# A two-layer diffusion backbone on one core: one adaLN sum a round in the first stage, attention biases asked for six units ahead, probabilities scaled on ScalarE, row norms with one PSUM bank per quarter and six chunks apart

## The chip, the cores and the metric

The kernel runs on one core of one Trainium2 chip. The metric is device time in microseconds (us). A core has five engines that run beside each other, each in its own order: TensorE (PE, with PEld for its weight loads), VectorE (DVE), ScalarE (ACT), GpSimd (POOL) and SyncE (SP). SP here does nothing but issue DMAs. An engine's queue is strictly in order, so an instruction that waits holds everything behind it. PSUM has eight banks of 512 fp32 numbers per partition.

## The reference

Two layers over 256 latent tokens of width 2048, with 256 context tokens. All is fp32.

- For each layer, six vectors come from `silu(cond) @ ada_w + ada_b` (adaLN): shift, scale and gate for the mixer, and the same for the FFN. Layer 0 needs shift and scale for latent tokens and for context tokens.
- Layer 0: `hx = rmsnorm(x) * g * (1 + scale) + shift`, the same for the context; Q, K, V and three convolution inputs from one projection; eight heads of neighbourhood attention. A query's scores are `q k / sqrt(128)` plus a relative position bias within its window, and plain scores for the 256 context keys; softmax over both; times V. Beside it a gated width-3 convolution. Both go through `w_out`, times the gate, onto x. Then a SwiGLU FFN (hidden width 5632) with its own norm and modulation.
- Layer 1: the same with a spatial-gating MLP in the place of attention. At the end an rmsnorm.

## The kernel before

**Products.** Every fp32 product is made of three fp32r products: each operand is split into a high part (`hi`, a copy by ScalarE that rounds) and a low part (`lo`, VectorE subtracts `hi`), and `mm3` (L172 to L175) issues hi by hi, hi by lo, lo by hi. Weights arrive as 512 KB chunks `raw` (four buffers), SP issues them, ScalarE makes `hl0`, VectorE makes `hl1` (six buffers each).

**First stage, 16 rounds** (the loop `for g in range(17)`, from L1092). A round loads four adaLN weight tiles `adaw` of 512 KB (`ada_tile`), a K chunk (512 KB) and a half V chunk (256 KB). TensorE multiplies the tiles by the two conditioning vectors (`row_part`, L336, into `aps`); VectorE copies the sums out (`asb`, L349); TensorE turns them into columns (`to_cols`, L362, `cps`). Rounds 0 to 7 make the scales and scale the inputs (`scale_step`); rounds 8 to 15, called shift rounds here, make the shifts and add them (`shift_step`, L415: a chain POOL, VectorE, ScalarE, VectorE for each of four pieces). In between TensorE multiplies the chunk of the round before, in four parts (`kv_part`). The 17th pass has only parts. The x and context columns are loaded by `load_x` at the rounds in `X_AT`; `row_sums` and `row_norms` make the row norms in round 6.

**The other adaLN sums.** The remaining ten sections are not products on TensorE: VectorE multiplies a 512 KB tile by silu(c) and sums it (`ada_compute`, L222). 320 such tiles are spread over the kernel by a running account (`ada["due"]`): `RATE_SH` tiles a shift round, `RATE_V1`, `RATE_EARLY` and `RATE_LATE` afterwards. They share a pool of three buffers (`adap`) with the first two of a round's four tiles.

**After that, units.** A unit is one weight chunk times one half of the tokens (t = 0 or 1): six matmuls. Chunks follow each other, t = 0 then t = 1. Around each of the three boundaries at which a row norm stands (before FFN 0, before the gMLP, before FFN 1) the last `LAG` chunks run for t = 0 and then for t = 1, and the first `LAG` of the next block likewise, so that a norm of one half has `LAG` units of the other half to hide in. Splits are emitted some 8 units ahead of their use, loads 13.

**Helpers that advance by units.** Attention, norms and evacuations are generators: each `yield` is one unit. `norm_T` takes one half's rows times their norm (`n`), turns each of four 512-wide quarters on TensorE (`flip`, T) and, in `fill` (E), applies scale and shift out of PSUM, 128 columns at a time: two by ScalarE (L791), two by VectorE (L793), into `hs`, and splits that into `tf`. `NORM_SEQ` lists which T and E stand in which step. `attention(h, t)` asks at t = 0 for the head's bias tile (`bias_tile`, two DMAs by SP with rows of 64 numbers, and a mask added by POOL, L688), waits three units, and then makes scores (`s`), adds the bias on VectorE (L701), takes the maximum, exponentials, reciprocals of the sums, and scales the probabilities on VectorE (L712); three units later TensorE transposes them (`pt`, L515). `ATT_AT` gives the units at which the 16 half heads start.

Of the kernel before, what the change touches and what calls it, by code (L numbers as in the profile page):

```python
# [32 lines left out]

LAG = 5
TW, TWA = 4, 3
HI_LEAD, DMA_LEAD, LEAD_IN = 8, 13, 14
RATE_SH, RATE_V1, RATE_EARLY, RATE_LATE = 1.5, 1.25, 0.88, 0.6
HOMES = {0: (1, 2, 1, 2), 1: (0, 0, 0, 1), 2: (0, 0, 1, 2)}  # L40
LEAD_AT = range(-14, -8), range(-8, -3), range(-3, 0)
X_AT = {0: (0,), 1: (1, 2), 2: (3, 4), 3: (5, 6), 4: (7,)}
FIRST_WAIT, KV_WAIT, X1_WAIT, ROW_WAIT = 2, 3, 4, 6
QUIET, LN_QUIET = (10, 5), (32, 39)
N_SPARE, SPARE_LEAD = 2, 12
# [3 lines left out]
def seq(text):  # L49
    return [[(a[0], int(a[1])) for a in step.split()] for step in text.split(",")]  # L50


NORM_SEQ = seq("T0 T1, E0 E1, T2 T3, E2 E3"), seq("T0, E0 T1, E1 T2, E2 T3, E3")
ACT_N = 1,
ATT_AT = (20, 6), (83, 5)
B_RAW, B_HL, B_ADA, B_STG = 4, 6, 3, 7


# [1 line left out]
def tile_backbone(  # L60
# [53 lines left out]
    def tp_tile(name):  # L114
        return tpp.tile([P, 512], F32, tag="tp", name=name)
# [572 lines left out]
        nc.gpsimd.tensor_tensor(out=ball, in0=ball, in1=mask.unsqueeze(1).to_broadcast([P, 6, GRID]), op=ALU.add)  # L688

    def attention(h, t):  # L690
        if t == 0:
            bias_tile(h)
            for _ in range(3):
                yield
        bias = BIAS[h][:, 2 - 2 * t:6 - 2 * t]
        sp = tp_tile("s")
        nc.tensor.matmul(sp, QT[h // 4, t][:, 128 * (h % 4):128 * (h % 4) + 128], kT(h), start=True, stop=True)
        yield
        s = stage("s")
        nc.scalar.copy(s[:, 256:512], sp[:, 256:512])  # L700
        nc.vector.tensor_tensor(out=s[:, 0:256], in0=sp[:, 0:256], in1=bias.rearrange("p r c -> p (r c)"),  # L701
                                op=ALU.add)
        yield
        mx = tiny.tile([P, 1], F32, tag="mx", name="mx")
        nc.vector.tensor_reduce(out=mx, in_=s, axis=AX.X, op=ALU.max, negate=True)
        yield
        sm = tiny.tile([P, 1], F32, tag="sm", name="sm")
        nc.scalar.activation(s, s, AF.Exp, bias=mx, accum_out=sm)
        yield
        rs = tiny.tile([P, 1], F32, tag="rs", name="rs")  # L710
        nc.vector.reciprocal(rs, sm)
        nc.vector.tensor_scalar(s, s, rs, None, op0=ALU.mult)  # L712
        yield from wait(TWA)
        tp = transpose4(s, "pt")
        yield
        pt = stage("pts")
        copy(h, pt, tp)
        yield from wait(TWA)
        av = tp_tile("av")
        for i in range(4):  # L720
            nc.tensor.matmul(av[:, 0:128], vv(h, i), pt[:, 128 * i:128 * i + 128],
                             start=(i == 0), stop=(i == 3))
        yield
        dh, dl = (MIX[0][:, k, h, 128 * t:128 * t + 128].rearrange("p (r c) -> p r c", c=GRID) for k in range(2))
        hi_part(dh, rev(av[:, 0:128], 2))
        yield
        lo_part(dl, rev(av[:, 0:128], 2), dh)
# [35 lines left out]
    def norm_T(key, t, l, part, T):  # L763
        assert ada["done"] >= 32 * (1 + max(ada_plan.index((l, sec)) for sec in ((0, 1), (3, 4))[part == "ffn"]))
        r = rms(key, t)
        ns = [stage("n") for _ in range(4)]
        for q in range(4):
            xq = X1[0][:, t, 512 * q:512 * q + 512]
            if q in ACT_N:
                nc.scalar.activation(ns[q], xq, AF.Copy, scale=r)  # L770
            else:
                nc.vector.tensor_scalar(ns[q], xq, r, None, op0=ALU.mult)
        for _ in range(NORM_WAIT):
            yield
        tps = {}

        def flip(q):
            tps[q] = [tp_tile("ntp")[:, 0:256] for _ in range(2)]
            for j in range(4):
                nc.tensor.transpose(tps[q][j // 2][:, 128 * (j % 2):128 * (j % 2) + 128],  # L780
                                    ns[q][:, 128 * j:128 * j + 128], ident)

        def fill(q):
            h, lw = quad(T, 4 * q, t)
            hs = stage("hs").rearrange("p (i k t) -> p i k t", i=2, k=2)
            for j in (0, 2, 1, 3):
                kt = 4 * q + j
                a, b = A[l, part][:, kt:kt + 1], SH[l, part][:, kt:kt + 1]
                src = tps[q][j // 2][:, 128 * (j % 2):128 * (j % 2) + 128]
                if j < 2:  # L790
                    nc.scalar.activation(hs[:, 0, j], src, AF.Identity, bias=b, scale=a)  # L791
                else:
                    nc.vector.tensor_scalar(hs[:, 1, j - 2], src, a, b, op0=ALU.mult, op1=ALU.add)  # L793
            for k in range(2):
                ks = slice(2 * k, 2 * k + 2)
                hi_part(h[:, ks], hs[:, k])
                lo_part(lw[:, ks], hs[:, k], h[:, ks])

        for step in NORM_SEQ[t]:
            for what, q in step:  # L800
                (flip if what == "T" else fill)(q)
            yield
# [71 lines left out]
    T1 = []  # L874
# [192 lines left out]
            if next(g, gens) is gens:  # L1067
                gens.remove(g)

    att_at = {}  # L1070
    for half, (u, step) in enumerate(ATT_AT):
        for k in range(8):
            att_at[4 * N_V1 + u + step * k] = (4 * half + k // 2, k % 2)

    quiet = [(b - QUIET[0], b + QUIET[1]) for b in bounds[:-1]]
    quiet.append((bounds[1] + LN_QUIET[0], bounds[1] + LN_QUIET[1]))
# [22 lines left out]
    for g in range(17):  # L1099
# [9 lines left out]
        if blk:  # L1109
# [1 line left out]
            for q in range(4):  # L1111
                row_part(aps, tiles[q], 4 * q)
            asb = row_done(aps, 256)
        if g >= 8:
            while ada["loaded"] < min(ada["done"] + 1, 14):
                ada_load()
        if g == 4:
            nc.gpsimd.dma_start(s_b, c_row.partition_broadcast(P))
        if g > 0:
# [1 line left out]
        if g == 16:  # L1121
            for u in LEAD_AT[1]:
                leads(u)
        if blk:
            cps = to_cols(asb, 2)
            if g == 0:
                pair = [split_tiles(r) for r in raw]
                held[0] = [[w.rearrange("p (j n) -> p j n", j=2) for w in p] for p in pair]
                scale_step(g, cps, [lambda j=j: [split_half(r, p, j) for r, p in zip(raw, pair)] for j in range(2)])
            elif g < 8:  # L1130
                scale_step(g, cps)
            else:
                shift_step(g - 8, cps, rb)
            if g > 0:
                held[g] = [split(r) for r in raw]
        if g > 1:
            kv_part(4 * g - 3)
        if g == 6:
            diag = row_sums()
        if g > 1:  # L1140
            kv_part(4 * g - 2)
        if g > 0:
            kv_part(4 * g - 1)
        if g == 6:
            rb = row_norms(diag)
        for s in X_AT.get(g, ()):
            squares(s)
# [2 lines left out]
        if 8 <= g < 16:  # L1150
            ada_ticks(RATE_SH)
        if g == 15:
            for u in LEAD_AT[0]:
                leads(u)
    KV[1] = big_f32("kv1")
# [1 line left out]
    kv_done(*acc_ps[1], ks1, 256)  # L1157
    for u in LEAD_AT[2]:
        leads(u)
    nc.vector.tensor_copy(cpad[:, :, 0:2], Sm)  # L1160

    for u in range(len(units)):
        leads(u)
# [4 lines left out]
        go(run(ci, t, hi, lo))  # L1168
        if i + 1 in starts:
            go(starts[i + 1](t))  # L1170
        if u in att_at:
            go(attention(*att_at[u]))
        if not any(a <= i < b for a, b in quiet):
# [76 lines left out]
```

## Time and profile before

| | |
|---|---|
| three runs | 2372.53 us median, 2369.86 to 2373.77 |
| the profiled execution | 2374.91 us, of which the trace's span is 2373.1 us |
| PE busy | 2311.2 us, 97% of the span |
| VectorE, ScalarE, GpSimd busy | 1611.7, 1009.6, 85.1 us |
| moved by DMA | 623.45 MB, 263 GB/s on average |
| granted TensorE clock, mean | 0.992 of full speed |

The profile is read from TensorE outwards: a busy PE at a full granted clock can't be helped by this change, so what counts is where PE is idle, where its clock is below 1.00, and which wait ends last there. Start times are in us from the start of the span. "A <- B" is an operation that writes A and reads B.

### The profile page before, as it was taken

The page shows a single profiled execution, that of the slowest core. Times are in us where ns is not written, and L with a number is a line of the kernel's source. Part 1 is how long each engine was busy: PE and PEld are TensorE (multiplying, and loading weights), DVE is VectorE, ACT ScalarE, POOL GpSimd, SP SyncE. Part 2 cuts the span into 40 slices and gives each one's busy share as a digit, 9 for nine tenths or more (in the row PEclk, how much of TensorE's full clock was granted, in tenths as well). Part 3 has the DMA queues.
Part 4 walks back from the last instruction along what each step waited for, and adds up shares of the span by engine and source line. Part 5 has one row for each costly group of instructions (what it writes and reads, how often), then busy time and mean ns, then how long its engine had stood idle before and what let it go on. Part 6 is the DMA issues. An engine that isn't in the chain of part 4 may idle for free.

```text
span 2373.1 us, 29680 instructions
## 1 busy us (share of the span) xinstructions
PE 2311.2 (97%) x11022; PEld 1883.9 (79%) x11022; DVE 1611.7 (68%) x2171; ACT 1009.6 (43%) x1268; POOL 85.1 (4%) x109
## 2 busy tenths in 40 slices
PE   8988999999999999999999999999999999999998
PEld 5766777778788888888888788887888888888886
DVE  4554579889776777777777778777774554455445
ACT  4322245444544434443444545446444344444443
POOL 3121000000000000000000000000000000000001
PEclk9998999999999999999999999999999999999999
DMA  9666888889688888878877688885876665655563
GB/s 353 239 248 244 295 278 281 279 307 362 222 292 313 307 297 323 310 287 305 325 289 286 209 300 321 281 299 183 317 272 216 204 192 182 194 195 190 183 195 133
DMA packets 184113, 623.45 MB, mean 263 GB/s; under 512 B 25952, under 2 KB 32288, under 8 KB 183584
## 3 DMA queue, kind: packets, MB, share of 16 engines
q1 hardware_dynamic: 181840, 614.71, 73.7%
q0 software_dynamic: 1840, 6.33, 0.8%
q8 instruction: 86, 1.41, 0.2%
q10 hardware_dynamic: 288, 0.52, 0.1%
q14 instruction: 59, 0.48, 0.1%
HBM read 619.35 MB, written 2.13 MB: 262 GB/s over the span
## 4 chain that ended last, share of the span: by engine, by line
PE 87%; DVE 5%; DMA 4%; issue 2%; ACT 1%; POOL 1%; SPq 0%; POOLq 0%; ACTq 0%; DVEq 0%
PE mm L173 25%; PE mm L175 25%; PE mm L174 25%; DMA bias<-in_rpb_dram 3%; DVE hl L522 1%; PE k L173 1%; PE k L174 1%; PE k L175 1%; PE aps L336 1%; DMA adaw<-in_ada_sh_dram 1%; DVE adaw L222 1%; PE htp L515 1%; PE v L173 1%; PE v L174 1%; PE v L175 1%
## 5 line engine op out<-in xcount | busy, mean ns | idle before, releaser
L519 ACT ACTIVATE hl<-raw 128x1024 fp32r<-128x1024 f32 x722 | 756.7, 1059 | 819.9 <-PE mm L175 626.6
L522 DVE TENSOR_TENSOR hl<-raw,hl 128x1024 fp32r<-128x1024 f32 x722 | 872.5, 1222 | 333.4 <-ACT hl L519 332.3
L173 PE MATMUL mm<-hl,tf 128*128 128x512 f32 x1392 | 545.5, 392 | 0.0
L175 PE MATMUL mm<-hl,tf 128*128 128x512 f32 x1392 | 542.0, 389 | 0.0
L174 PE MATMUL mm<-hl,tf 128*128 128x512 f32 x1392 | 541.8, 389 | 0.0
L175 PEld LDWEIGHTS mm<-hl,tf 128*128 128x128 f32 x1392 | 261.3, 188 | 54.8
L173 PEld LDWEIGHTS mm<-hl,tf 128*128 128x128 f32 x1392 | 261.3, 188 | 53.6 <-issue 0.6
L174 PEld LDWEIGHTS mm<-hl,tf 128*128 128x128 f32 x1392 | 261.4, 188 | 53.2
L173 PE MATMUL mm<-hl,hid 128*128 128x512 f32 x704 | 275.1, 391 | 0.0
L175 PE MATMUL mm<-hl,hid 128*128 128x512 f32 x704 | 274.0, 389 | 0.0
L174 PE MATMUL mm<-hl,hid 128*128 128x512 f32 x704 | 274.0, 389 | 0.0
L222 DVE CUSTOM_DVE_ANT_0 adaw<-adaw,s_b,colt 128x1024 f32<-128x1024 f32 x160 | 204.4, 1277 | 0.8 <-DMA adaw<-in_ada_rest_dram 0.5
L222 DVE CUSTOM_DVE_ANT_0 adaw<-adaw,s_b 128x1024 f32<-128x1024 f32 x160 | 194.7, 1217 | 7.8 <-DMA adaw<-in_ada_rest_dram 7.8
L175 PEld LDWEIGHTS mm<-hl,hid 128*128 128x128 f32 x704 | 132.1, 188 | 27.7
L174 PEld LDWEIGHTS mm<-hl,hid 128*128 128x128 f32 x704 | 132.2, 188 | 27.1
L173 PEld LDWEIGHTS mm<-hl,hid 128*128 128x128 f32 x704 | 132.2, 188 | 26.9
L740 DVE TENSOR_TENSOR g<-mm,row 128x512 f32<-128x512 f32 x64 | 44.0, 687 | 99.0 <-PE mm L175 99.0
L173 PE MATMUL mm<-hl,tx 128*128 128x512 f32 x256 | 109.0, 426 | 0.0
L175 PE MATMUL mm<-hl,tx 128*128 128x512 f32 x256 | 100.2, 391 | 0.0
L174 PE MATMUL mm<-hl,tx 128*128 128x512 f32 x256 | 100.1, 391 | 0.0
L173 PE MATMUL mm<-hl,tm 128*128 128x512 f32 x248 | 97.9, 395 | 0.0
L175 PE MATMUL mm<-hl,tm 128*128 128x512 f32 x248 | 96.6, 390 | 0.0
(254 smaller groups left out, 2465.9 us busy)
## 6 DMA issues: line engine op xcount, KB each, us to landing
adaw<-in_ada_rest_dram SPq DMA_DIRECT2D x320, 512.0 KB, 6.0
raw<-in_w_gate_dram SPq DMA_DIRECT2D x176, 512.0 KB, 4.8
raw<-in_w_up_dram SPq DMA_DIRECT2D x176, 512.0 KB, 5.0
raw<-in_w_down_dram SPq DMA_DIRECT2D x176, 512.0 KB, 4.6
raw<-in_w_in_dram SPq DMA_DIRECT2D x88, 512.0 KB, 6.5
raw<-in_w_out_dram SPq DMA_DIRECT2D x64, 512.0 KB, 5.7
raw<-in_w_odd_in_dram SPq DMA_DIRECT2D x64, 512.0 KB, 5.5
adaw<-in_ada_sc_dram SPq DMA_DIRECT2D x32, 512.0 KB, 6.9
```

The lines of the kernel that those rows point to most:

```text
L173: nc.tensor.matmul(ps, lh, rh, start=first, stop=False)
L174: nc.tensor.matmul(ps, lh, rl, start=False, stop=False)
L175: nc.tensor.matmul(ps, ll, rh, start=False, stop=last)
L222: nc.vector.tensor_tensor_reduce(out=raw, in0=raw, in1=s_b[:, 1024 * hf:1024 * hf + 1024], scale=1.0, scalar=0.0 if hf else adab(l, sec, k ...
L336: nc.tensor.matmul(aps[32 * g:32 * g + 32, 0:w.shape[2]], cpad[:, kt, :], w[:, j], start=(kt < 4), stop=(kt >= 12), tile_position=(0, 32 * g))
L515: nc.tensor.transpose(tp[:, 128 * j:128 * j + 128], src512[:, 128 * j:128 * j + 128], ident)
L519: nc.scalar.activation(dst, src, AF.Copy)
L522: nc.vector.tensor_tensor(out=dst, in0=src, in1=hi.bitcast(F32), op=ALU.subtract)
L740: nc.vector.tensor_tensor(out=g, in0=ps, in1=GROW[l, sec, nb], op=ALU.mult)
```

## The change

- First stage: `RATE_SH` goes from 1.5 to 1: one adaLN sum a shift round, where two and one took turns. Its tile is asked for right after the round's own loads. `RATE_EARLY` goes from 0.88 to 0.93. The x and context columns are loaded over rounds 0 to 5 (two pairs in rounds 2 and 5) where it was 0 to 4; row sums and norms stand in round 7. In round 15 the chunk is split before the shifts, the shifts are copied to `cpad` there, and two sum tiles are asked for in the 17th pass.
- Attention: `bias_tile` is called six units before its head starts, and the wait of three units goes; the half heads start two units later and every 6 (5) units. The scaling by the reciprocals moves to ScalarE, one unit after the reciprocals.
- Norms: `LAG` goes from 5 to 6. A quarter's four transposes go into one PSUM bank where they had two; the steps are `T0 T1, E0 T2, E1 T3, E2, E3` for both halves.

```diff
-LAG = 5
+LAG = 6
-RATE_SH, RATE_V1, RATE_EARLY, RATE_LATE = 1.5, 1.25, 0.88, 0.6
+RATE_SH, RATE_V1, RATE_EARLY, RATE_LATE = 1, 1.25, 0.93, 0.6
-X_AT = {0: (0,), 1: (1, 2), 2: (3, 4), 3: (5, 6), 4: (7,)}
+X_AT = {0: (0,), 1: (1,), 2: (2, 3), 3: (4,), 4: (5,), 5: (6, 7)}
-NORM_SEQ = seq("T0 T1, E0 E1, T2 T3, E2 E3"), seq("T0, E0 T1, E1 T2, E2 T3, E3")
+NORM_SEQ = seq("T0 T1, E0 T2, E1 T3, E2, E3")
-ATT_AT = (20, 6), (83, 5)
+ATT_AT, BIAS_LEAD = ((22, 6), (85, 5)), 6
...
     def attention(h, t):
-        if t == 0:
-            bias_tile(h)
-            for _ in range(3):
-                yield
...
         nc.vector.reciprocal(rs, sm)
-        nc.vector.tensor_scalar(s, s, rs, None, op0=ALU.mult)
+        yield
+        nc.scalar.activation(s, s, AF.Copy, scale=rs)
...
         def flip(q):
-            tps[q] = [tp_tile("ntp")[:, 0:256] for _ in range(2)]
-            for j in range(4):
-                nc.tensor.transpose(tps[q][j // 2][:, 128 * (j % 2):128 * (j % 2) + 128],
-                                    ns[q][:, 128 * j:128 * j + 128], ident)
+            tps[q] = transpose4(ns[q], "ntp")
...
-                src = tps[q][j // 2][:, 128 * (j % 2):128 * (j % 2) + 128]
+                src = tps[q][:, 128 * j:128 * j + 128]
...
+            if k % 2 == 0:
+                bias_at[4 * N_V1 + u + step * k - BIAS_LEAD] = 4 * half + k // 2
...
-        if g >= 8:
-            while ada["loaded"] < min(ada["done"] + 1, 14):
-                ada_load()
+        if 8 <= g < 16:
+            ada_load()
...
         if g == 16:
             for u in LEAD_AT[1]:
                 leads(u)
+            ada_load()
+            ada_load()
...
-            else:
+            elif g < 15:
                 shift_step(g - 8, cps, rb)
             if g > 0:
                 held[g] = [split(r) for r in raw]
+            if g == 15:
+                shift_step(7, cps, rb)
...
-        if g == 6:
+        if g == 7:
             diag = row_sums()
...
         if g == 15:
+            nc.vector.tensor_copy(cpad[:, :, 0:2], Sm)
             for u in LEAD_AT[0]:
                 leads(u)
...
-    nc.vector.tensor_copy(cpad[:, :, 0:2], Sm)
...
+        if u in bias_at:
+            bias_tile(bias_at[u])
```

Three places of the order. First SP's queue in the shift rounds, before: the second sum tile of round 8 (`adaw_1146`), the four tiles of round 9 (`adaw_1149` to `_1155`), its K and V chunks, its sum tile, the first tile of round 10.

```order
L212 DMA adaw_1146<-in_ada_rest0_dram 128x1024 [waits DMAHW1_49,DMAHW0_49,PE_49]
L356 DMA adaw_1149<-in_ada_sh_dram 128x1024 [waits DMAHW2_49,PE_49]
L356 DMA adaw_1151<-in_ada_sh_dram 128x1024 [waits DMAHW1_49,PE_49]
L356 DMA adaw_1153<-in_ada_sh_dram 128x1024 [waits DMAHW3_49]
L356 DMA adaw_1155<-in_ada_sh_dram 128x1024 [waits DMAHW4_49]
L169 DMA raw_1157<-in_w_in_dram 128x1024 [waits DMAHW5_49,DVE_49]
L303 DMA raw_1159<-in_w_in_dram 128x2x256 [waits DMAHW6_49,DVE_49]
L212 DMA adaw_1180<-in_ada_rest0_dram 128x1024 [waits DMAHW7_49,DMAHW2_49,PE_49]
L356 DMA adaw_1272<-in_ada_sh_dram 128x1024 [waits DMAHW0_49,DVE_49]
```

With two of the three buffers held by the two sum tiles of round 8, `adaw_1149` and `adaw_1151` have the same buffer: the second waits until TensorE has used the first. Now, from round 8's one sum tile on, round 9 and the first two tiles of round 10:

```order
L212 DMA adaw_1048<-in_ada_rest0_dram 128x1024 [waits DMAHW7_49,PE_49]
L356 DMA adaw_1146<-in_ada_sh_dram 128x1024 [waits DMAHW1_49,DMAHW0_49,PE_49]
L356 DMA adaw_1148<-in_ada_sh_dram 128x1024 [waits DMAHW2_49,PE_49]
L356 DMA adaw_1150<-in_ada_sh_dram 128x1024
L356 DMA adaw_1152<-in_ada_sh_dram 128x1024 [waits DMAHW3_49]
L169 DMA raw_1154<-in_w_in_dram 128x1024 [waits DMAHW4_49,DVE_49]
L303 DMA raw_1156<-in_w_in_dram 128x2x256 [waits DMAHW5_49,DVE_49]
L212 DMA adaw_1177<-in_ada_rest0_dram 128x1024 [waits DMAHW6_49,DMAHW0_49,PE_49]
L356 DMA adaw_1269<-in_ada_sh_dram 128x1024 [waits DMAHW7_49,DMAHW1_49,PE_49]
L356 DMA adaw_1271<-in_ada_sh_dram 128x1024 [waits DVE_49]
```

Now a sum tile takes the buffer of the same round's first tile once TensorE has read it; the next round's first tile takes the buffer of the second; its second tile takes the buffer of the sum tile of the round before, which VectorE has to have summed.

Second, ScalarE in the first fill of the first norm, before:

```order
L770 ACTIVATE n<-x_4523,r 128x512 [waits Pool_49]
L519 ACTIVATE hl_5154<-raw 128x1024 [waits DMAHW2_49,PE_49,Activation_49]
L519 ACTIVATE hl_5166<-raw 128x1024 [waits DMAHW3_49,PE_49,Activation_49]
L791 ACTIVATE hs<-ntp,SH_ffn,A_ffn 128x128 [waits PE_49,Activation_49]
L791 ACTIVATE hs<-ntp,SH_ffn,A_ffn 128x128
L519 ACTIVATE tf_5132<-hs 128x2x128 [waits Activation_49]
L519 ACTIVATE tf_5132<-hs 128x2x128 [waits DVE_49]
```

And now, ScalarE and then VectorE in the same fill:

```order
L785 ACTIVATE hs<-ntp,SH_ffn,A_ffn 128x128
L785 ACTIVATE hs<-ntp,SH_ffn,A_ffn 128x128 [waits DVE_49]
L519 ACTIVATE tf_5126<-hs 128x2x128 [waits Activation_49]
L519 ACTIVATE tf_5126<-hs 128x2x128 [waits DVE_49]
```

```order
L522 TENSOR_TENSOR hl_5154<-raw,hl_5146 128x1024 [waits DMAHW1_49,Activation_49]
L522 TENSOR_TENSOR hl_5164<-raw,hl_5156 128x1024 [waits DMAHW2_49,Activation_49]
L522 TENSOR_TENSOR hl_5184<-raw,hl_5166 128x1024 [waits DMAHW3_49,Activation_49]
L787 TENSOR_SCALAR hs<-ntp,A_ffn,SH_ffn 128x128 [waits PE_49,Activation_49]
L787 TENSOR_SCALAR hs<-ntp,A_ffn,SH_ffn 128x128 [waits Activation_49]
L522 TENSOR_TENSOR tf_5126<-hs,tf_5126 128x2x128 [waits Activation_49] x2
L522 TENSOR_TENSOR hl_5208<-raw,hl_5186 128x1024 [waits DMAHW4_49,PE_49]
```

In the one bank the two engines now take turns: VectorE's first waits for ScalarE's first, ScalarE's second for VectorE's first, VectorE's second for ScalarE's second. Before, ScalarE and VectorE each had a bank and waited for TensorE alone. Between the rows `n` and the first fill VectorE has three splits (`hl`) now as before; a fourth (`hl_5208`), which stood behind the second half's norm, now stands between the first fill and the second.

Third, VectorE in the first half head of attention, before and now:

```order
L701 TENSOR_TENSOR s<-s,bias 128x256
L222 ISA adaw,acc<-adaw,s_b 128x1024
L222 ISA acc 128x1
L522 TENSOR_TENSOR hl_2821<-raw,hl_2807 128x1024
L705 TENSOR_REDUCE mx<-s 128x1
L522 TENSOR_TENSOR hl_2845<-raw,hl_2833 128x1024
L711 RECIPROCAL rs<-sm 128x1
L712 TENSOR_SCALAR s<-s,rs 128x512
```

```order
L697 TENSOR_TENSOR s<-s,bias 128x256
L222 ISA adaw,acc<-adaw,s_b 128x1024
L222 ISA acc 128x1
L701 TENSOR_REDUCE mx<-s 128x1
L522 TENSOR_TENSOR hl_2803<-raw,hl_2793 128x1024
L222 ISA adaw,acc<-adaw,s_b,colt 128x1024
L222 ISA acc 128x1
L707 RECIPROCAL rs<-sm 128x1
L522 TENSOR_TENSOR hl_2828<-raw,hl_2818 128x1024
```

The scaling has left VectorE; splits (`hl`) and adaLN sums (`adaw`) still stand behind the row that adds the bias, so whatever that row waits for, they wait for too.

## Rows read from the trace of the kernel before

**Rows 1.** The page's busy time, its share of the span and the instructions.
```profile
PE 2311.2 (97%) x11022; PEld 1883.9 (79%) x11022; DVE 1611.7 (68%) x2171; ACT 1009.6 (43%) x1268; POOL 85.1 (4%) x109
```
**Rows 2.** Waits of PE over the span: total us, times, longest.
```profile
PE aps L336 <- DMA adaw<-in_ada_sh_dram: 18.4, 12, 3.9
PE pt L515 <- DVE s L712: 8.0, 8, 2.4
PE ntp L780 <- ACT hs L791: 7.1, 9, 0.9
...
PE ntp L780 <- DVE hs L793: 3.8, 6, 0.7
PE aps L336 <- DMA adaw<-in_ada_sc_dram: 2.2, 5, 0.8
```
**Rows 3.** Chain that ended last: start, us, what; rounds 8, 10, after the stage.
```profile
100.23 1.86 PE aps L336 x32
...
130.15 1.86 PE aps L336 x32
...
232.36 0.86 PE aps L344 x16
```
**Rows 4.** Windows: length, busy us (count) PE PEld DVE ACT POOL, PEclk, DMA share, GB/s.
```profile
45.00:55.00 10.00, 10.00 (x82) 8.05 (x81) 5.94 (x11) 5.49 (x10) 5.09 (x4) 1.00 1.02 383
111.00:119.00 8.00, 3.53 (x34) 0.77 (x32) 6.36 (x11) 2.56 (x6) 0.73 (x1) 0.75 0.76 273
119.00:130.00 11.00, 11.00 (x62) 9.11 (x54) 4.05 (x11) 2.88 (x5) 3.53 (x5) 0.87 0.83 325
1850.00:1900.00 50.00, 50.00 (x223) 41.39 (x222) 26.20 (x27) 19.11 (x18) 0.00 (x0) 1.00 0.58 188
```
**Rows 5.** Timeline of SP's queue, tiles 2 to 4 of round 9: start, us, what.
```profile
111.84 1.28 SPq L356 DMA_DIRECT2D adaw<-in_ada_sh_dram  x3
```
**Rows 6.** Timeline of PE, round 9's products [idle before <- what ended it].
```profile
111.14 0.64 PE L336 MATMUL aps<-adaw,cpad 128*32 128x256 f32 x8
...
115.67 1.08 PE L336 MATMUL aps<-adaw,cpad 128*32 128x256 f32 x8 [3.90 <-DMA adaw<-in_ada_sh_dram]
```
**Rows 7.** Timeline of VectorE: end of round 8; round 10 from copy to second sum.
```profile
113.54 1.27 DVE L432 COPY ks<-k 128x512 f32<-128x512 f32 x2
...
133.31 0.42 DVE L349 COPY asb<-aps 128x256 f32<-128x256 f32 x1
134.72 0.35 DVE L418 TENSOR_SCALAR Sm<-cps,colt 128x2 f32<-128x2 f32 x2 [0.99 <-PE cps L362]
...
144.22 1.27 DVE L222 CUSTOM_DVE_ANT_0 adaw<-adaw,s_b,colt 128x1024 f32<-128x1024 f32 x1
```
**Rows 8.** The bias tile: its instructions (ns min/median/max), who waited, landing times.
```profile
L688 POOL TENSOR_TENSOR bias<-bias,mask x8: 992/1009/1020, 326.5 to 499.0; 128x384 f32<-128x384 f32 x8
...
  DVE s L701: 31.5, 8
...
DMA to landing us min/median/max: 6.4/8.4/11.3
```
**Rows 9.** Timeline of VectorE at the first norm.
```profile
598.77 0.69 DVE L740 TENSOR_TENSOR g<-mm,row 128x512 f32<-128x512 f32 x1 [2.50 <-PE mm L175]
...
603.03 3.49 DVE L522 TENSOR_TENSOR hl<-raw,hl 128x1024 fp32r<-128x1024 f32 x3
606.44 0.72 DVE L793 TENSOR_SCALAR hs<-ntp,A_ffn,SH_ffn 128x128 f32<-128x128 f32 x2
...
609.54 0.68 DVE L740 TENSOR_TENSOR g<-mm,row 128x512 f32<-128x512 f32 x1
```
**Rows 10.** Groups by form: count, busy us, mean ns, idle before.
```profile
L791 ACT ACTIVATE hs<-ntp,SH_ffn,A_ffn 128x128 f32<-128x128 f32 x32 | 12.6, 443 | 0.0
L793 DVE TENSOR_SCALAR hs<-ntp,A_ffn,SH_ffn 128x128 f32<-128x128 f32 x32 | 11.6, 402 | 0.0
L770 ACT ACTIVATE n<-x,r 128x512 f32<-128x512 f32 x6 | 4.3, 724 | 5.3 <-POOL r L760 5.3
```

More of the change, by code (lines that the diff above doesn't have):

```diff
@@ L797, in fill @@
                 lo_part(lw[:, ks], hs[:, k], h[:, ks])
-        for step in NORM_SEQ[t]:
+        for step in NORM_SEQ:
             for what, q in step:
@@ L1068, in advance @@
                 gens.remove(g)
-    att_at = {}
+    att_at, bias_at = {}, {}
     for half, (u, step) in enumerate(ATT_AT):
@@ L1143, in tile_backbone @@
             kv_part(4 * g - 1)
-        if g == 6:
+        if g == 7:
             rb = row_norms(diag)
```

## The prediction

> **What bounds the kernel now.** The page comes first: TensorE is busy for 2311.2 of 2373.1 us [rows 1]. The change takes no matmul away, so what it can win is the 61.9 us in which TensorE is idle and what it loses at a low clock. The list of TensorE's waits comes next [rows 2]: 18.4 us for adaLN tiles of the shift rounds, 8.0 for scaled probabilities (`pt`), 10.9 at the norms (`ntp`, 7.1 and 3.8), 2.2 for tiles of the scale rounds. These 39.5 us are what the edits aim at; the rest lies at the start and the end of the kernel, which no edit touches. The windows come third [rows 4]: after the wait of round 9 the granted clock is 0.75 and then 0.87, and TensorE gets through 62 matmuls in 11 us where an undisturbed stretch has 82 in 10. So a wait here costs more than its own length. The timelines then say why each wait is there.
>
> **Shift rounds.** Round 8 takes 111.14 - 100.23 = 10.91 us, rounds 8 and 9 together 130.15 - 100.23 = 29.92 [rows 3, 6]. A round with a wait thus takes 19.0 us, 8.1 more than its work: some 4.6 us idle (18.4 over four such rounds, rows 2) and 3.5 at the low clock. The wait's cause stands in SP's rows: tiles 2 to 4 of round 9 are asked for at 111.84 [rows 5], when TensorE has used the first one (111.14 + 0.64, rows 6), because the two sum tiles of the round before hold the other two buffers. By the new order no tile of a round waits for another tile of that round. Its second one waits for a sum one round and more earlier, which VectorE has behind it.
>
> What is late next is VectorE. Round 10 goes from its copy at 133.31 to the end of the first of its two sums at 144.22 [rows 7]: 10.91 us with one sum, as much as TensorE's round. I take 11.0 a round. Round 9 is longer: VectorE's copies out of the first half's banks (from 113.54, 1.27 us and one more pair, rows 7) come after TensorE has finished the products of round 9 (111.14 plus 1.9, rows 3, 6), and TensorE needs these banks. Before, that lay under the wait for tiles; now it shows: 2.4 us of wait and some 1.1 of catching up, 3.5. The 17th pass has a round's parts without the products, 10.9 - 1.9 = 9.0. From round 8 to the first products after the stage: 8 x 11.0 + 3.5 + 9.0 = 100.5, against 232.36 - 100.23 = 132.1 before [rows 3]. That is 31.6; I take 31. In it is the earlier copy to `cpad`, and round 15's split ahead of its shifts. Bounds: 8 x 10.9 + 9.0 gives 36. At the other end, a round moves 3.25 MB (3.41 million bytes: four tiles, a chunk and a half, a sum tile), which takes 8.9 us at the 383 GB/s of an undisturbed stretch and 12.5 at 273 [rows 4]; at 12.5 the term is 19.
>
> The four sums that leave the stage are made later by VectorE, which is busy 68% of the time [rows 1] and not what TensorE waits for there: nothing, as long as that cover holds.
>
> **Scale rounds.** Half a megabyte less is asked for in round 1, ahead of round 2's tiles; at 383 GB/s [rows 4] they land 1.4 us sooner. The columns that come later have to be there one round on. Of the 2.2 us of waits [rows 2] I take 1; bounds 2.2 and, if the columns come a little late once, -2.
>
> **Attention.** A unit is six matmuls; 223 in 50 us [rows 4] makes it 1.35 us. Before, the bias had four units from the load to the add, 5.4 us, and needs 8.4 to land and 1.0 on POOL [rows 8]: 4.0 us short, and VectorE did wait 31.5 us in eight times, 3.9 each [rows 8]. Now it has seven, 9.45 us against 9.4: the median just fits, the slowest (11.3 + 1.0) is 2.9 late. So VectorE's wait falls from 31.5 to perhaps 8, and `pt` has a unit more. The scaling costs ScalarE 0.72 us (the same shape and kind) [rows 10], with three units, 4 us, to spare; behind it stand splits, whose weights may be late. Of the 8.0 us I take 7. One thing gets tighter: the last half head starts at unit 120 (85 + 5 x 7) of 128 and has its low part one unit before `w_out` needs it, where it had four. I take 1 us for that, 0 to 4 as bounds. Net 6; bounds 8 and -8 (each of 16 half heads 1 us late on ScalarE).
>
> **Norms.** TensorE waits 3.6 us per boundary, for the banks of fills that are late. VectorE makes them late: from the first half's residual at 598.77 to the second half's at 609.54 it does the norm, three splits (3.49) and two fills without a gap [rows 9]. Six chunks apart, TensorE comes a unit later, and no transpose waits for a fill of its own half. But the order shows the two engines taking turns in a fill: 2 x 0.443 + 2 x 0.402 = 1.69 us [rows 10] where ScalarE's pair and VectorE's ran side by side (0.89). With the two splits behind it (0.4 each) VectorE is held some 2.3 us, where two fills took 609.54 - 606.44 = 3.1. And a fourth split, 1.15, now stands between the two. From 606.44 on: 2.3 + 1.15 + 2.1 puts the second half's residual at 612.0. TensorE is through with that half at 598.7 + 6 x 1.35 + 16 transposes (some 2) = 609, and three units later, at 613, wants its first quarter, which comes 3.4 us after the residual starts (the norm takes 4.3 in all, 598.77 to 603.03, rows 9): 615.4. That is a new wait of 2.4 us, and I add 0.5 for fills that come late after it. 2.9 for 3.6, three times: a gain of 2. Bounds: all 10.9 gone, and, with 24 fills by 0.8 us each on TensorE's path, -19. I take the value in between because VectorE is the engine that sets the end here in the rows before.
>
> The Trainium skill, "PSUM — Partial Sum Buffer", section "PSUM bank collisions raise a hardware error", says that two engines that touch one bank in the same partitions must be kept apart by semaphores, reads against reads too. It speaks against this edit: by it the fill is serial whatever the units say, and the term is the 2 above, where without the rule (a fill as before, 0.89) it would be some 9. The waits in the order agree; no row of before shows a fill in one bank.
>
> Six chunks at once also fill all six split buffers, so the last of six is split 5 units ahead (6.8 us) where it was 6. ScalarE and VectorE need some 1.1 us each for it. Nothing, unless VectorE is as far behind as it is in attention now.
>
> **Sum.** 31 + 1 + 6 + 2 = 40 us. The profiled execution took 2374.91 for a span of 2373.1; the median of the runs is 2372.53, and I subtract from that: 2332.5, say 2332.
>
> **The rivals.**
> - The shift rounds are paced by DMA or by VectorE at 12.5 us: 12 us of the gain are missing, 2344. For it: VectorE's round and TensorE's are equal, so any delay shows, and 80% of what DMA showed is asked for. Against: the rounds before 66 us run at 383 GB/s with TensorE full [rows 4].
> - The fills come late, or ScalarE does in attention. Half of the fills' 19 us on the path, and nothing won in attention: 2 + 9 and 6 less, some 2348. For it: VectorE is already the late one. Against: the extra chunk.
> - Everything goes: norms 10.9 for 2, attention 8: 2321.
> - Slower than before: the clock stays at its low level (1.2 of 2.4 GHz). VectorE's round equals TensorE's, so TensorE may have a short idle piece in every round. At half the rate a round is 21.8 us; eight, the last pass at 18 and 3.5 make 196 for 132, 64 us more, less the 9 won elsewhere: 2428. It decides at rounds of some 15.9 us: 8 x 15.9 + 9 + 3.5 is the 132 and the 9. For it: the clock did fall behind the waits of 3.9 us. Against: it is 1.00 in the full stretch from 45 us [rows 4], and the short waits at the norms.
> - The Trainium skill, "TensorE: Matmul & The Clock Gate", section "HAM oscillation — how this bites in real kernels", tells of a kernel that waits for DMA in every tile and runs cold each time; by that rule this is what the old rounds did, and the new ones would do it only if a wait of that kind stayed in each.
> - The change doesn't do what it says: the second tile still comes late in every round, all eight take 19.0, 152 + 9 for 132, 29 more, 9 won elsewhere: 2393. Against: the order.
>
> **Chances and range.** Forecast 0.56 (2324 to 2339), slow rounds 0.19, late fills 0.12, everything 0.09, clock or tiles late in each round 0.03, and 0.01 for nothing at all. The range is 2317 to 2350: it takes in the first four and most of the unknown bounds. Under 0.2%, 4.7 us, a measurement of this kernel can't tell a change from none. Faster 0.95, within 0.2% 0.02, slower 0.03.
>
> **What would show it.** In the profile after: rounds 8 to 15 some 11 us apart with no wait for `adaw` tiles and a granted clock of 1.00 from 100 to 200 us; VectorE's wait for the bias below 10 us and TensorE's for `pt` near 1; at the norms no wait of `ntp` for a fill's bank in the first half, but one for `n` at the second. I am wrong if the rounds are over 12 us, if the clock dips again, or if waits at the norms grow beyond 11 us.

## The result, and the profile after

The changed kernel takes 2348.21 us (median of four runs, 2346.37 to 2348.85), the kernel before 2371.2 beside it: a ratio of 0.9904, 95% interval 0.9887 to 0.9921. That is 23 us less where 39 were expected between these medians (2332); the direction and the range held, 16 us of the gain are missing. The profiled executions are further apart (spans 2344.6 and 2373.1, 28.5 us), since the one of before took 2374.91 us and the one of after 2346.37, each a little off its median, to either side. Parts are therefore compared by medians, mechanisms by traces.

The page's busy line of the changed kernel [rows 1]:

```profile
PE 2303.8 (98%) x11022; PEld 1884.7 (80%) x11022; DVE 1606.8 (69%) x2155; ACT 1022.8 (44%) x1284; POOL 86.4 (4%) x109
```

TensorE is idle for 2344.6 - 2303.8 = 40.8 us, before 61.9: 21.1 us less. The same matmuls take 7.4 us less of busy time; that fits the granted clock, 0.995 on average for 0.992. Next the waits of PE over the whole span, changed kernel (total us, times, longest), to be read beside [rows 2]:

```profile
PE ntp L515 <- DVE n L769: 9.4, 4, 2.7
PE vh L320 <- ACT zr L296: 5.3, 1, 5.3
PE gp L247 <- DVE t L244: 3.5, 2, 2.8
PE av L718 <- DVE mixa L522: 2.7, 1, 2.7
PE aps L336 <- DMA adaw<-in_ada_sc_dram: 2.3, 5, 0.7
...
PE av L718 <- DVE rs L707: 1.1, 1, 1.1
PE mm L173 <- ACT tf L519: 1.0, 4, 0.3
PE pt L515 <- ACT s L709: 0.7, 2, 0.5
PE s L693 <- ACT pts L432: 0.7, 1, 0.7
PE av L718 <- DVE pts L432: 0.4, 1, 0.4
```

The 18.4 us for `adaw` tiles of the shift rounds are gone, `pt` is down from 8.0 to 0.7, and no fill's bank is waited for. New or larger are the rows `n` at the norms and the tiles that the fills make (`tf`, 1.0, and `tm`, 0.4), the sums of a gate (`gp`, 0.4 before), VectorE in attention's products with V (`av`, 4.2 in three rows), and ScalarE in its scores (`s`, 0.7). Windows of PE, changed kernel (length, PE busy and matmuls, granted clock, DMA share, GB/s): the shift rounds to the first products after the stage, behind the gate, then the three norms.

```profile
100.20:198.40 98.20, 97.23 (x727) 1.00 0.81 292
300.00:307.00 7.00, 7.00 (x25) 0.76 0.64 173
560.00:600.00 40.00, 35.25 (x158) 0.96 0.44 145
1300.00:1350.00 50.00, 46.79 (x211) 0.97 0.46 148
1590.00:1640.00 50.00, 47.03 (x210) 0.93 0.49 173
```

Before, the same norms stood some 30 us later; windows around them, same columns:

```profile
560.00:650.00 90.00, 86.31 (x391) 1.00 0.74 263
1300.00:1400.00 100.00, 96.37 (x436) 1.00 0.69 242
1600.00:1700.00 100.00, 96.21 (x438) 1.00 0.68 240
```

The clock is 1.00 in the shift rounds now [rows 4 for before], and below it at four places where it was 1.00 before (behind the old gate too, from 320 to 327 us). The part of full speed that is missing, times the length, is what each costs: 1.7 us behind the gate (0.24 x 7), 1.6, 1.5 and 3.5 at the norms.

The chain that ended last shows the stage (start, us, what; rounds 8, 10 and 15, and the end of the stage) [rows 3]:

```profile
100.22 1.04 PE aps L336 x16
...
124.11 1.86 PE aps L336 x32
...
178.97 1.86 PE aps L336 x32
198.43 0.79 PE aps L344 x16
```

Rounds 10 to 15 are (178.97 - 124.11)/5 = 10.97 us apart; the stage ends 34 us earlier (198.4 for 232.4).

### The profile page after: what moved, and what is told of

The parts are those of the page before. It is cut to its first block, busy times and chain, and to the rows that moved or that the text cites. A ratio compares the mean times of both kernels' runs of the same rounds, so it can differ in the third digit from the quotient of the medians.

```text
span 2344.6 us, 29683 instructions
## 1 busy us (share of the span) xinstructions
PE 2303.8 (98%) x11022; PEld 1884.7 (80%) x11022; DVE 1606.8 (69%) x2155; ACT 1022.8 (44%) x1284; POOL 86.4 (4%) x109
## 2 busy tenths in 40 slices
DMA packets 184113, 623.45 MB, mean 266 GB/s; under 512 B 25952, under 2 KB 32288, under 8 KB 183584
## 4 chain that ended last, share of the span: by engine, by line
PE 85%; DVE 6%; DMA 4%; issue 2%; ACT 2%; POOL 0%; SPq 0%; POOLq 0%; DVEq 0%; ACTq 0%
PE mm L173 25%; PE mm L175 25%; PE mm L174 25%; DVE hl L522 2%; DVE adaw L222 1%; PE k L173 1%; PE k L174 1%; PE k L175 1%; DMA adaw<-in_ada_sc_dram 1%; DMA adaw<-in_ada_rest_dram 1%; PE aps L336 1%; PE htp L515 1%; PE v L173 1%; DMA raw<-in_w_in_dram 1%; PE v L174 1%
## 5 line engine op out<-in xcount | busy, mean ns | idle before, releaser
L174 PE MATMUL mm<-hl,tx 128*128 128x512 f32 x256 | 100.5, 393 | 0.0
```

The source lines that it names most:

```text
L174: nc.tensor.matmul(ps, lh, rl, start=False, stop=False)
```

## The experiments

Medians in us; the runs of before beside them had medians of 2371.2 to 2373.0. Each ratio is to before, with its 95% interval.

| kernel | median (runs) | ratio |
|---|---|---|
| changed kernel | 2348.2 (2346.4 to 2348.9) | 0.9904 [0.9887, 0.9921] |
| stage alone | 2343.0 (2342.4 to 2343.8) | 0.9878 [0.9864, 0.9893] |
| norms undone | 2341.6 (2340.9 to 2343.5) | 0.9875 [0.9858, 0.9891] |
| second fill later | 2350.9 (2350.4 to 2352.5) | 0.9913 [0.9898, 0.9927] |
| gate later | 2340.3 (2337.8 to 2342.7) | 0.9867 [0.9852, 0.9881] |
| six chunks, two banks | 2343.1 (2341.5 to 2346.5) | 0.9877 [0.9863, 0.9890] |
| pairs in a fill | 2337.3 (2335.7 to 2340.0) | 0.9852 [0.9838, 0.9865] |
| bias by GpSimd's queue | 2340.4 (2339.2 to 2342.0) | 0.9864 [0.9851, 0.9877] |
| stage alone, gate later | 2338.5 (2337.9 to 2342.4) | 0.9859 [0.9846, 0.9873] |
| norms undone, gate later | 2336.9 (2334.7 to 2338.4) | 0.9859 [0.9841, 0.9877] |
| the same, bias by GpSimd | 2333.9 (2329.9 to 2335.4) | 0.9844 [0.9827, 0.9861] |
| all three mended | 2330.6 (2327.8 to 2333.1) | 0.9832 [0.9816, 0.9848] |
| the same, scaling on VectorE | 2330.5 (2325.5 to 2333.3) | 0.9830 [0.9810, 0.9849] |

### The three parts, one after the other

**Stage alone**: the changed kernel with attention and norms as before; what stays of the change is `RATE_SH`, `RATE_EARLY`, `X_AT` and the code of the stage.

```diff
-LAG = 6
+LAG = 5
-ATT_AT, BIAS_LEAD = ((22, 6), (85, 5)), 6
+ATT_AT = (20, 6), (83, 5)
...
-        yield
-        nc.scalar.activation(s, s, AF.Copy, scale=rs)
+        nc.vector.tensor_scalar(s, s, rs, None, op0=ALU.mult)
...
-            tps[q] = transpose4(ns[q], "ntp")
+            tps[q] = [tp_tile("ntp")[:, 0:256] for _ in range(2)]
...
```

> Only the first stage is changed (with the account's rates that go with it); attention and norms are those of the kernel before. Theory: the stage's gain stands by itself. In the traces the first products after the stage begin at 232.4 us before and at 198.4 in the changed kernel, 34 us; so 2371 - 34 = 2337 us, or up to 2342 if the late gate line (2.85 us of wait of TensorE and 3.4 us at half the clock) comes with the four sums that leave the stage. Rival: VectorE's backlog in attention takes part of it back; then 2345 or more.

2343.0: it won 28.4 us, not 34. That is 1 us beyond the theory's upper end (2342) and short of the rival's 2345. Waits of PE in it:

```profile
PE gp L247 <- DVE t L244: 4.5, 2, 3.9
...
PE pt L515 <- DVE s L712: 3.9, 6, 1.2
```

Behind the wait of 3.9 us the granted clock is 0.52 from 300 to 307 us: 3.4 more. So the gate came with the stage edits.

**Norms undone**: the changed kernel with `LAG = 5`, two banks per quarter and the old steps.

```diff
-LAG = 6
+LAG = 5
-            tps[q] = transpose4(ns[q], "ntp")
+            tps[q] = [tp_tile("ntp")[:, 0:256] for _ in range(2)]
...
```

> The changed kernel with the norms of before (five chunks, two banks per quarter). Theory: the norm edits cost time. TensorE waited 10.9 us at the norms before at a full clock; in the changed kernel it waits 9.4 for n and 1.4 for tf, and 13.65 us at half the clock (6.8 lost) follow, 17.6 in all; so 6.7 us come back: 2341.5 us, no granted clock below 1.00 at the norms. Rival, the prediction's own term: the norm edits won 2 us, then 2350. Beside the run with the stage alone it also gives the worth of the attention edits: theory, none (the two within 2 us); prediction, 6 us.

2341.6, as the theory had it: 6.6 us come back, and the runs do not overlap with the changed kernel's. Windows of PE at the gate and the three norms, columns as above:

```profile
300.00:307.00 7.00, 7.00 (x26) 0.80 0.60 165
560.00:600.00 40.00, 36.33 (x171) 1.00 0.52 166
1300.00:1350.00 50.00, 46.33 (x214) 1.00 0.59 195
1590.00:1640.00 50.00, 46.18 (x210) 1.00 0.67 230
```

The waits of before are back at the norms (36.33 of 40 us busy at the first), but the clock is 1.00 at all three. Between the stage alone and this kernel lie the attention edits, 1.4 us, which the runs can't tell from none. The parts then are 28.4 + 1.4 - 6.6 = 23.2, against 32 + 6 + 2 in the prediction: 3.6, 4.6 and 8.6 are missing.

### The norms

In the changed kernel VectorE does this at the first norm (start, us, instruction, idle time before it and what ended it), beside [rows 9]:

```profile
565.90 0.68 DVE L737 TENSOR_TENSOR g<-mm,row 128x512 f32<-128x512 f32 x1
...
574.07 0.40 DVE L787 TENSOR_SCALAR hs<-ntp,A_ffn,SH_ffn 128x128 f32<-128x128 f32 x1
575.00 0.41 DVE L787 TENSOR_SCALAR hs<-ntp,A_ffn,SH_ffn 128x128 f32<-128x128 f32 x1 [0.53 <-ACT hs L785]
...
579.55 0.68 DVE L737 TENSOR_TENSOR g<-mm,row 128x512 f32<-128x512 f32 x1
```

From residual to residual it takes 13.65 us where before it took 10.77. And TensorE, same kernel:

```profile
583.11 1.64 PE L515 MATMUL ntp<-ident,n 128*128 128x128 f32 x8 [2.69 <-DVE n L769]
```

**Second fill later.**

```diff
-NORM_SEQ = seq("T0 T1, E0 T2, E1 T3, E2, E3")
+NORM_SEQ = seq("T0 T1, E0 T2, T3, E1, E2, E3")
```

> The changed kernel with the second fill of each half emitted one unit later (T0 T1, E0 T2, T3, E1, E2, E3). Theory: the second half's rows n are late because that fill (577.38 to 579.55 on VectorE) stands ahead of the second half's residual; it goes behind, n is 2.1 us earlier, TensorE's wait of 2.7 us falls to some 0.6 at each norm, and the clock stays at 1.00, so 3 x 2.1 and 6.8 us: 2335. Rival 1: the wait goes, but the clock was not tied to it: 2342. Rival 2: VectorE is late whatever the order, and TensorE waits for the fills (tf) in place of n: 2348 or more.

2350.9: my theory fell, the second rival came true. `n` of the second half is early enough, but the fill, now behind that whole norm on VectorE, is late for the products of the first half (waits of PE):

```profile
PE mm L173 <- ACT tf L519: 9.2, 3, 4.5
...
PE mm L173 <- ACT tm L519: 4.4, 1, 4.4
```

Three waits of 4.4 to 4.5 us stand where three of 2.7 stood. The order of the steps is not the trouble; VectorE is late whichever comes first.

**Six chunks, two banks**: the fills and steps of before, `LAG` still 6.

```diff
-            tps[q] = transpose4(ns[q], "ntp")
+            tps[q] = [tp_tile("ntp")[:, 0:256] for _ in range(2)]
...
```

> The changed kernel with the fills of before (two banks per quarter, old steps) but still six chunks apart. Theory: the one bank is what delays VectorE; with two banks a pair of fills takes 3.1 us of VectorE in place of 4.3, the second half's n comes 1.2 us earlier, its wait falls from 2.7 to 1.5 us without the clock falling behind it, while the waits for fills' banks of before (some 3 us a norm) come back: (1.5 + 3) x 3 = 13.5 for 17.6, 2344. Rival 1: six chunks are what costs (the fourth split ahead of the second half's residual), 2348. Rival 2: with six chunks the second half hides its fills, 2338, below the kernel with five.

2343.1: near the theory's 2344, and within the spread of five chunks with two banks (2341.6). Six chunks by themselves neither win nor cost, as far as these runs can tell. What cost the 5.1 us between this and the changed kernel is the single bank or the steps that came with it; the two were taken back together here.

**Pairs in a fill**: one bank, six chunks, but ScalarE does its two pieces and then VectorE its two.

```diff
-            for j in (0, 2, 1, 3):
+            for j in range(4):
```

> The changed kernel with a fill's four pieces in the order ScalarE, ScalarE, VectorE, VectorE, so the one bank changes hands once and not three times. Theory: VectorE waits some 0.5 us less in each fill (0.53 in the trace, once per fill), so n of the second half is 1.06 us earlier, its wait 1.6 us for 2.7, and the clock stays at 1.00: 3 x 1.06 and up to 6.8 us less, 2338 to 2345. Rival: VectorE's first piece now waits for two of ScalarE's, the fill ends where it did, 2348.

2337.3, 11 us below the changed kernel. Who waited for the other engine's `hs` (us, times), first in the changed kernel, then here:

```profile
  ACT hs L785: 23.0, 24
  DVE hs L787: 16.2, 28
```

```profile
  ACT tf L519: 10.2, 16
  DVE hs L787: 6.2, 10
  ACT tm L519: 5.1, 8
```

With one handover VectorE waits 10 us less. ScalarE no longer waits at the bank; it waits for VectorE's pieces when it splits them, 15.3 us for 23.0. And TensorE (waits, then windows at the norms):

```profile
PE ntp L515 <- DVE n L769: 7.3, 4, 2.2
```

```profile
560.00:600.00 40.00, 36.94 (x176) 1.00 0.48 158
1300.00:1350.00 50.00, 47.92 (x225) 1.00 0.57 194
1590.00:1640.00 50.00, 47.80 (x212) 0.97 0.66 241
```

Norms cost 7.3 + 0.03 x 50 = 8.8 us, against 10.8 + 6.6 = 17.4 in the changed kernel (9.4 for `n`, 1.4 for the tiles that the fills make, the clock) and 10.9 before. Of the 8.6 us between the two, 5.1 are the clock. So the single bank by itself does not cost time here; changing hands three times in a fill did.

### The gate

**Gate later.** The sums of a gate end in a small product on TensorE (`gp`) that stands in its queue one unit behind the last sum; here four.

```diff
         nc.vector.tensor_tensor(out=t32[:, 0:KT], in0=acc[:, 0], in1=acc[:, 1], op=ALU.add)
-        yield
+        yield from wait(4)
```

> The changed kernel with TensorE's turn of the gate sums (gp) put three units later after the last sum. Theory: TensorE's queue stood 2.85 us for a sum that is not needed yet, and 3.4 us at half the clock (1.7 lost) followed; both go, and 0.7 us of a second such wait: 2343. Rival: VectorE is as late as before, and the next thing that TensorE takes from it (probabilities, the products with V) waits in its place: 2348.

2340.3, 8 us less where 5 were expected; the spans of the two profiles differ by 4.7. The wait is gone, and so is the low clock at 300 us:

```profile
300.00:307.00 7.00, 7.00 (x35) 1.00 0.59 158
```

The waits for `n` are as in the changed kernel (9.5 us, four times, up to 2.7), but the windows at the three norms read

```profile
560.00:600.00 40.00, 35.07 (x159) 0.96 0.42 139
1300.00:1350.00 50.00, 45.67 (x211) 1.00 0.50 167
1590.00:1640.00 50.00, 46.55 (x206) 0.97 0.58 206
```

so the clock did not fall at the second one, and less at the third: 3.1 us in place of 6.6. In attention it fell once more, 0.96 from 440 to 480 us behind a wait at `av` of 2.62 us, where the changed kernel has 1.00 behind one of 2.69. Part of what this run won is thus the clock at places that the edit does not touch.

**Stage alone, gate later**: the same edit on the stage alone.

```diff
-        yield
+        yield from wait(4)
```

> The first stage alone with TensorE's turn of the gate sums three units later. Theory: what the stage alone lacks of its 34 us (it won 28.4) is the gate line, 4.5 us of wait and 6.8 us at half the clock (3.4) in its trace; 2343.0 - 7.9 = 2335. Rival: VectorE's lateness costs the same at the next place, 2342.

2338.5, between theory and rival: 4.5 of the 7.9 us came back. Where the rest went is not settled. The profiled execution took 2342.35, the slowest of the four and as long as that of the stage alone (2342.39); in it TensorE waits elsewhere:

```profile
PE pt L515 <- DVE s L712: 7.5, 7, 2.4
```

It was 3.9 without this edit. That VectorE had caught up while TensorE stood for the gate is my reading of it, and not shown.

### Attention

VectorE's waits from 250 to 560 us, changed kernel [rows 8]:

```profile
DVE adaw L222 <- DMA adaw<-in_ada_rest_dram: 23.0, 9, 5.0
...
DVE s L697 <- ACT s L696: 8.6, 4, 3.9
```

A bias tile lands in 7.7 us (median; 8.4 before). VectorE never waits for the bias (31.5 us before), but 23.0 for sum tiles, where the same view of before has 5.0. Why these are late is in SP's queue, changed kernel; its waits from 250 to 560 us and a stretch of its timeline:

```profile
SPq L687 <- PE av L718: 6.7, 3, 5.1
...
SPq L687 <- DVE pts L432: 3.4, 1, 3.4
```

```profile
444.10 0.33 SPq L1081 DMA_DIRECT2D raw<-in_w_in_dram  x1
449.07 1.27 SPq L687 DMA_DIRECT2D bias<-in_rpb_dram  x2
450.39 0.60 SPq L212 DMA_DIRECT2D adaw<-in_ada_rest_dram  x1
```

The bias tile takes one of the seven staging buffers. Asked for six units early, it has to wait for one (the rows name the readers of other tiles as what ended the wait), and SP stands until it is free; the sum tile behind it leaves at 450.39, VectorE waits 4.97 us for it and starts at 460.29, and TensorE waits 2.69 us for VectorE at 461.78.

**Bias by GpSimd's queue.**

```diff
-            nc.sync.dma_start(ball[64 * r2:64 * r2 + 64], src)
+            nc.gpsimd.dma_start(ball[64 * r2:64 * r2 + 64], src)
```

> The changed kernel with the bias tiles asked for by GpSimd's queue in place of SP's. Theory: SP's queue stands for a free staging buffer at the early bias request (444.4 to 449.1 us), the sum tiles behind it come late, VectorE waits 2.98 and 4.97 us for two of them, and TensorE 4.9 us for VectorE at the products with V and the scores; with the bias in another queue these waits go: 2344. Rival: the tiles are late because the bias's short rows hold the DMA engines, whoever asks; then VectorE's waits for adaw stay and the time is 2348.

2340.4, 8 us less. The same 623.45 MB move, in fewer packets (178481 for 184113) that take no less time (76.4% of the DMA engines' span in the two queues, 75.4% before this edit), and VectorE's wait for sum tiles (250 to 560 us) falls to

```profile
DVE adaw L222 <- DMA adaw<-in_ada_rest_dram: 6.5, 7, 4.2
```

so it was the queue and not the DMA engines. GpSimd's queue now stands for these buffers, up to 48.1 us at a time, and VectorE waits 3.9 us for two bias tiles. TensorE's waits at `av` fall from 4.2 to 0.4, those for the gate from 3.5 to 2.4, and the clock doesn't fall behind the latter. Not all of the 8 us belong to the bias: the waits for `n` are the same 9.4 us, but the clock at the three norms was 0.96, 1.00 and 0.97 in the same windows, 3.1 us in place of 6.6, and this edit does not touch them (over the four runs the mean granted clock is 0.997 to 0.998, in the changed kernel 0.993 to 0.996). Why the clock fell less there is open. Without those 3.5 the gain is some 4.4, near the theory's 4.

### Put together

**Norms undone, gate later.**

```diff
-LAG = 6
+LAG = 5
...
-        yield
+        yield from wait(4)
...
-            tps[q] = transpose4(ns[q], "ntp")
+            tps[q] = [tp_tile("ntp")[:, 0:256] for _ in range(2)]
```

> Stage and attention edits of the change, norms of before, gate sums three units later: beside the stage alone with the gate later (2338.5 us) it differs by the attention edits only. Theory: they win the 7.5 us that TensorE waited for pt there and the 1.7 of clock, and pay some 5 us at the products with V, where VectorE is late for sum tiles: 2335. Rival, the prediction's term of 6 us with no new wait: 2332.5.

Beside the stage alone with the gate later the ratio is the same (0.9859 both): with the bias in SP's queue the attention edits win nothing. 2336.9 is neither 2335 nor 2332.5; 1.7 us lie between the medians.

**The same, bias by GpSimd's queue.**

```diff
-            nc.sync.dma_start(ball[64 * r2:64 * r2 + 64], src)
+            nc.gpsimd.dma_start(ball[64 * r2:64 * r2 + 64], src)
```

> The same with the bias asked for by GpSimd's queue. Theory: the early bias request in SP's queue is what the attention edits pay with; without it the waits at the products with V (some 4.5 us) go: 2330 to 2331. Rival: with the gate out of the way SP is no longer held at that place, 2335.

2333.9: 3.0 us less, in the direction of the theory, but nearer the rival's 2335 than its 2331, with runs that overlap by 0.7 us. The attention edits come to 4.6 us in this form by the medians, 3.6 by the ratios, nearer the 6 of the prediction.

**All three mended**: the changed kernel with pairs in a fill, the gate later, the bias by GpSimd's queue.

```diff
-            for j in (0, 2, 1, 3):
+            for j in range(4):
...
-        yield
+        yield from wait(4)
...
-            nc.sync.dma_start(ball[64 * r2:64 * r2 + 64], src)
+            nc.gpsimd.dma_start(ball[64 * r2:64 * r2 + 64], src)
```

> The changed kernel with three things mended: a fill's pieces in the order ScalarE twice, VectorE twice; gate sums three units later; bias by GpSimd's queue. Against the kernel just named it differs by the norms (six chunks, one bank). Theory: six chunks and one bank with one handover wait 9.0 us at the norms (7.3 and 1.7 at the low clock, as measured) where five and two banks wait 10.9: 2328 to 2329. Rival: six chunks leave VectorE one split later at the norm and win nothing, 2330 to 2331.

2330.6 us, 17.6 below the changed kernel and 40.6 below before (ratio 0.9832, interval 0.9816 to 0.9848). The figure is the rival's, but both counted from a kernel above of 2330 to 2331, and that one took 2333.9. Against it this one is 3.3 us lower with overlapping runs, so that its norms win something is likely but not settled. Waits of PE:

```profile
PE ntp L515 <- DVE n L769: 7.8, 4, 2.2
```

**The same, scaling on VectorE.**

```diff
-        yield
-        nc.scalar.activation(s, s, AF.Copy, scale=rs)
+        nc.vector.tensor_scalar(s, s, rs, None, op0=ALU.mult)
```

> The same as the last, but the probabilities are scaled on VectorE again, with the reciprocals. Theory: the early bias removes the waits for pt, the place of the scaling matters little: at most 2 us more, 2328 to 2331. Rival: VectorE's queue is what makes pt late, and most of the 7 us comes back: 2334.

2330.5, no difference: TensorE waits 1.6 us for `pt` in it and 1.3 in the kernel above, against 8.0 before. So the early bias, with the half heads' new places, is what freed `pt`; the engine that scales does not matter.

## Why the prediction was right or wrong

- **Shift rounds: right.** 100.5 us were worked out from round 8 to the end of the stage, 98.2 it took: rounds of 10.97 (11.0), round 9 some 13.0 (14.5; a bump of 2 us where 3.5 were taken, of which 0.85 is a wait for `asb`, which stands behind the copies out of the banks on VectorE), the last pass 198.43 - 178.97 - 10.97 = 8.5 (9.0). No tile was waited for and the clock stayed at 1.00. VectorE's round, as long as TensorE's, held nothing up, and the rivals with slow or cold rounds fell. Scale rounds: 2.3 us for 2.2, the 1 us did not come.
- **"Nothing, as long as that cover holds": wrong**, and it is the first step that failed. Four sums fewer in the stage move the end of the first gate's 32 sums from 88.0 us after the stage (320.4 - 232.4) to 101.1 (299.5 - 198.4), into the heads of attention, where VectorE is late. TensorE takes part there: `gp` is on its queue. The stage alone lost 4.5 us and 3.4 of clock on it. I had asked what VectorE's sums cost VectorE, and not which engine takes their result and when.
- **Attention: the waits went as worked out, the price was not seen.** VectorE's wait for the bias went to 0 (8 expected), TensorE's for `pt` from 8.0 to 0.7 (7 expected to go). The failed step is the bias tile's move: only its landing time was counted, not the queue it was moved in, nor the buffer that it holds three units longer (seven from the load to the add, for four). SP stood 10.1 us for that buffer (6.7 + 3.4), and `av` and `s` cost TensorE 4.9 us. So 1.4 us in place of 6; with the bias in GpSimd's queue it was 4.6, or 3.6 by the ratios.
- **Norms: the wait was right, its price wrong.** The new wait for `n` was put at 2.4 us and measures 2.69; VectorE's time between the residuals at 13.2 (612.0 - 598.77) and measures 13.65. The sum, 2.9 for 3.6, charged it at its length. But behind one wait of 2.7 us the clock fell at all three norms, 6.6 us in all, and behind the short ones of before (up to 0.9, [rows 2]) it did not. The prediction had the rule that a wait costs more than its length from the shift rounds [rows 4], and did not apply it here. The wait of `n` at the first half too (1.29 us at the first norm) was not foreseen. The taking of turns was: VectorE waited 16.2 us for ScalarE in 28 pieces of fills, ScalarE 23.0 for VectorE in 24, and with one handover 6.2 and none at the bank. By the Trainium skill, "PSUM — Partial Sum Buffer", section "PSUM bank collisions raise a hardware error", two engines must be kept from touching one bank in the same partitions at the same time. The program does so here, and these waits are what it cost; no run here shows the collision itself.
- **The rivals.** "Late fills" named 2348 and hit the time by two parts of which one held: nothing was won in attention. The norms lost too, though not by late fills (`tf` 1.0 us) but by late `n` and the clock. With the gate, the fills and SP's stall mended the time is 2330.6, near the sum's 2332. By the ratios the stage, attention and the norms then win 33.4, 3.6 and 2.8 us, where the sum had 32, 6 and 2; each of the last two is within the spread of the runs. The range held for the changed kernel because it was wide enough for 16 us of costs that the sum put at nothing, not because they were foreseen.

## What to carry to other kernels

A wait of the engine that sets the time is charged with its length and with the clock that may fall behind it; here one longer wait mostly cost more than several short ones of the same sum. Two engines that share a bank should change hands once, not piece by piece. A request that is moved ahead in an in-order queue takes its buffer as much earlier, and everything behind it waits for that buffer: count free buffers at the new place before counting landing times. And where work is moved off one stage, look for who takes its result, not only for who does it.

## What the runs showed of the hardware

Whether the clock falls behind a wait of 2 to 3 us is not fixed. Behind waits for `n` of up to 2.7 us it fell at three of three norms in the changed kernel, and with the gate later, or with the bias by GpSimd's queue, at two of three with the same waits. With pairs, at up to 2.2 us, it fell at one of three, and so it did with all three mended; with the scaling on VectorE and the same waits at two of three. Each fall cost 1.5 to 3.5 us beside the wait. Short waits are not always free either: with six chunks and two banks it fell at the third norm (0.83 from 1590 to 1600 us) behind waits of 0.72, 0.20 and 0.71 us close together, while in the traces of the norms of before, with waits of up to 0.9 us, it never did. What decides it is not shown.

The Trainium skill, "TensorE: Matmul & The Clock Gate", section "HAM oscillation — how this bites in real kernels", describes a kernel whose clock falls behind the wait for DMA in every tile. The old shift rounds agree (0.75 behind a wait of 3.90 us, [rows 4, 6]); at the norms here, where TensorE waits for VectorE, the clock fell behind some waits and not behind others.
